# Banded self-attention in a decoder trunk: scores from split operands, transposes and values one tile further back, and the output projection's first tiles in two parts

## The chip, the core and the metric

The kernel runs on one core of a Trainium2 chip. Its engines take their instructions from queues of their own and wait for each other through semaphores: TensorE (PE in the profile; PEld are its weight loads) multiplies matrices into PSUM, VectorE (DVE), ScalarE (ACT) and GpSimd (POOL) work on tiles, and SyncE (SP) issues most of the transfers from memory. The metric is the time of one execution on the device in microseconds, here called us.

## The reference

A decoder trunk of two layers works on 256 positions of width 2048. Layer 0 mixes with a gated convolution and a state-space model; layer 1, the odd one, with the sliding-window attention below. After the mixer each layer has a cross-attention into 256 memory tokens and a gated MLP. Everything is float32. The change is in layer 1's mixer and in the table of its position bias:

```python
def swa_sink_attention(h, w_qkv, b_qkv, sinks, rel_bias, w_out):
    z = h @ w_qkv + b_qkv
    q, k, v = jnp.split(z, [N_Q_HEADS * HEAD_DIM, (N_Q_HEADS + N_KV_HEADS) * HEAD_DIM], axis=-1)
    ...
    kb, vb = with_prev(k), with_prev(v)
    s = jnp.einsum('bnqkgd,bnskd->bnkgqs', q, kb).astype(jnp.float32) * (HEAD_DIM ** -0.5)
    ...
    s = jnp.where(valid[None, :, None, None], s + bias[None, None], NEG_INF)
    ...
    p = jax.nn.softmax(jnp.concatenate([s, sink], axis=-1), axis=-1)[..., :-1]
    o = jnp.einsum('bnkgqs,bnskd->bnqkgd', p.astype(vb.dtype), vb)
    return o.reshape(Bsz, L, N_Q_HEADS * HEAD_DIM) @ w_out
```

There are 32 query heads of width 64 and 4 key heads. Queries come in two blocks of 128. A query sees the block of keys it is in and the block before, and of these the 128 latest positions. The first block has no block before it. So a head needs scores of 128 by 256 for the second block and of 128 by 128 for the first, 384 columns in all. A learned sink per head adds one more term to the softmax's sum.

## The kernel before

**Activations** lie with their features on the 128 partitions: a tensor of width 2048 is 16 tiles (KT = 16) of 128 features by 256 positions (T = 256).

**Split products.** A large product in float32 is made of three cheaper ones. Each operand is written as a high part in the type float32r and a low part, the rest. For weights `wload` loads a raw tile (L82, SyncE's queue, three buffers), ScalarE makes the high part of up to 1024 columns at a time (L90) and VectorE the low part (L91), with four buffers each. An activation tile `op` holds its high and its low half side by side (512 columns; `split`, L74 and L75, or `split_gain`, L67 and L68). For each k-tile `mm_hi` multiplies the weight's high part with all 512 columns (L105), and `mm_lo` the low part with the high half, 256 columns (L110). The two halves of the result bank are added later.

**`gemm`** runs over output tiles of 128 features. `start` loads a tile's weights and issues its matmuls: all of `mm_hi`, then the function `half`, then all of `mm_lo`. `finish` calls `evac`, which takes the result out of PSUM, and then the function `after`. With `pre` and `late` the first `pre` tiles leave their last `late` k-tiles for afterwards, which `held` collects. What `half`, `after` and `end` issue is wedged into the stream of matmuls at these places. The order on each engine is that of the program as far as the planner of the tile framework keeps it: it puts ready work ahead of work that waits.

**The odd mixer** (`odd_mixer`) first makes keys `kT` (two tiles; `evac_k` adds the bias on ScalarE, L690) and values `vt` (L719). Then a `gemm` over 16 q tiles makes two query heads in each. Its `evac_q` adds the two halves (L160 on ScalarE, L161 on VectorE), multiplies with the normalisation on GpSimd (L726), and adds the bias on ScalarE (L728), with the positions of each block in reverse order, so that a bias row can be read at a shifting offset. For each pair of heads j there are three steps:

- `scores(j)`: loads the bias from a table in memory (L737), 256 columns of each head; multiplies q and k as plain float32, 64 rows of the array for each head, with 256 columns for the second block (L742) and 128 for the first (L745), into two small banks; adds the bias on VectorE in four pieces (L747, L748); makes the softmax: maxima, exponentials on ScalarE with their sums (L757, L760), the sum with the sink (L761), its reciprocal (L762) and four multiplications with it (L765). The result is `s`.
- `transp(j)`: three transposes for each head on TensorE (L774) into two small banks, copied by ScalarE to `pT` (L777).
- `values(j)`: multiplies `vt` with `pT` in plain float32, 64 columns of the array for each head (L788), into a small bank, which `split` makes the next operand of `o_ops` (L789).

In q tile n, `half` issues `transp(n - 3)`, and `after` issues `scores(n - 1)` and `values(n - 3)`. Each plain float32 product is two instructions in the trace.

**The output projection** is a `gemm` over 16 tiles whose k-tiles are the 16 entries of `o_ops`. At its start 13 entries are there. `transp(13)` is issued ahead of it; its first three tiles hold back their last three k-tiles, and in them the dictionaries `halves` and `ends` issue what is left: `values(13)` and `scores(15)`, `transp(14)`, `values(14)`, `transp(15)`, `values(15)`. Its `evac` (`resid_evac`) adds both halves to the residual stream on VectorE (L288, L289), squares on ScalarE (L174), sums on GpSimd (L172), and splits the result for the next stage (L67, L68).

**The position bias** is made once, long before (`rel_bias_setup`): a row of 384 for each head, written to memory by one transfer (L676). A query's bias is a stretch of 256 of that row, at an offset that moves with the query.

**PSUM** is two pools of four banks each: `pp` for the results of `gemm` (the tag `ps`), `pm` for the small ones (`bank()`).

Of the kernel before, what the change touches and what calls it, by code (L numbers as in the profile page):

```python
# [22 lines left out]
P = 128  # L23
# [13 lines left out]
class Trunk:  # L37
# [623 lines left out]
    def rel_bias_setup(self):  # L661

        nc, I = self.nc, self.I
        with self.tc.tile_pool(name="rb", bufs=1) as pool:
# [10 lines left out]
            self.fd = self.dp.tile([32, 384], F32, name="fd")  # L675
            nc.scalar.dma_start(self.fd, f)  # L676

    def odd_mixer(self, xs):
# [3 lines left out]
        with tc.tile_pool(name="att", bufs=2) as pool:  # L682
            kT = [pool.tile([P, T], F32, name=f"kT{j}", tag=f"kT{j}", bufs=1) for j in range(2)]
            vt = pool.tile([P, 2, T], F32, name="vt", tag="vt", bufs=1)

            def evac_k(n, ps):
                z = self.t1()
                self.add_halves(z, ps)
                nc.gpsimd.tensor_tensor(z, z, self.rbc, op=ALU.mult)
                nc.scalar.activation(kT[n], z, AF.Identity, bias=self.k_b[:, n:n + 1])  # L690
# [32 lines left out]
            def evac_q(n, ps):  # L723
                z = self.t1()
                self.add_halves(z, ps)
                nc.gpsimd.tensor_tensor(z, z, rbc, op=ALU.mult)  # L726
                q = pool.tile([P, T], F32, name="q", tag="q", bufs=3)
                nc.scalar.activation(q.rearrange("p (b i) -> p b i", b=2)[:, :, ::-1], z.rearrange("p (b i) -> p b i", b=2), AF.Identity, bias=self.q_b[:, n:n + 1])  # L728
                qs[n] = q
# [3 lines left out]
            def scores(j):  # L733
                q = qs.pop(j)
                k = kT[j // 8]
                bias = pool.tile([P, 2, T], F32, name="bias", tag="bias", bufs=3)
                nc.sync.dma_start(bias, AP(tensor=self.fd.tensor, offset=self.fd.offset + 2 * j * 384, ap=[[1, P], [384, 2], [1, T]]))  # L737
                s = pool.tile([P, 2, 384], F32, name="s", tag="s", bufs=3)
                ps = [self.bank() for _ in range(2)]
                for hd in range(2):  # L740
                    r = slice(64 * hd, 64 * hd + 64)
                    nc.tensor.matmul(ps[hd][:, 0:T], lhsT=q[r, P:], rhs=k[r, :], start=True, stop=True)  # L742
                for hd in range(2):
                    r = slice(64 * hd, 64 * hd + 64)
                    nc.tensor.matmul(ps[hd][:, T:T + P], lhsT=q[r, :P], rhs=k[r, :P], start=True, stop=True)  # L745
                for hd in range(2):
                    v.scalar_tensor_tensor(s[:, hd, :T], ps[hd][:, :T], 0.125, bias[:, hd, :], op0=ALU.mult, op1=ALU.add)  # L747
                    v.scalar_tensor_tensor(s[:, hd, T:], ps[hd][:, T:T + P], 0.125, bias[:, hd, P:], op0=ALU.mult, op1=ALU.add)  # L748
# [13 lines left out]
                v.reciprocal(de, de)  # L762
                for hd in range(2):
                    for blk, sl in ((0, slice(0, T)), (1, slice(T, 384))):
                        v.tensor_scalar(s[:, hd, sl], s[:, hd, sl], de[:, blk, hd:hd + 1], None, op0=ALU.mult)  # L765
# [15 lines left out]
            def values(j):  # L781
                pts = sm.pop(j)
                po = self.bank()
# [7 lines left out]
            def after(n):  # L791
                if n >= 1:
                    scores(n - 1)
                if n >= 3:
                    values(n - 3)

            def half(n):
                if n >= 3:
                    transp(n - 3)
            self.gemm(lambda n: I["od_q"][n], range(16), xs, KT, evac_q, half=half, after=after)  # L800
            evac, nxt = self.resid_evac(G_XA + 1)
            halves = {0: lambda: (values(13), scores(15)), 1: lambda: values(14), 2: lambda: transp(15)}
            ends = {0: lambda: transp(14), 1: lambda: None, 2: lambda: values(15)}
            transp(13)
            self.gemm(lambda n: I["od_w_out"][n], range(16), _Lazy(o_ops), KT, evac, late=3, pre=3, half=lambda n: n in halves and halves[n](), end=lambda n: ends[n]())
# [296 lines left out]
```

## Time and profile before

| | |
|---|---|
| median of three runs | 2818.43 us |
| the three runs | 2815.97, 2818.43, 2819.57 us |
| the profiled execution, its own time | 2817.71 us |
| its span, from the first to the last instruction | 2815.9 us |
| granted TensorE clock, mean | 0.997 |
| the odd mixer's q tiles, from the first scores on | 1646.2 to 1764.8 us of the span |
| its first three output tiles | 1764.9 to 1788.6 us |
| transfers of od_w_out | 16 of 1024 KB, 4.8 us each to landing |

The profile is one execution. Between the span and the execution's own time lie 1.8 us in which no instruction of the program runs. A row of the costliest groups gives line, engine, operation, output from inputs, shapes and count, then the busy time, the mean nanoseconds of one, and the idle time of the engine just before, with what ended it. A row of the chain of waits gives start, length and what; the lengths add up to the time that passes.

### The profile page before, as it was taken

To read this page: it belongs to the slowest core of one execution; us is meant where nothing else is said; L and a number is where in the kernel's file an instruction comes from. 1 tells how busy PE (TensorE), PEld (TensorE's weight loads), DVE (VectorE), ACT (ScalarE), POOL (GpSimd) and SP (SyncE) were. 2 spreads that over 40 slices of the span, in tenths; PEclk is the share of its full clock that TensorE was granted. 3 is DMA by queue.
4 is the path that set the end of the run, shared out by engine and by line. 5 is a ranking of instruction groups with operands and counts; after the bars stand their busy time and mean duration, and the time that the engine had idled before them with its cause. 6 is when DMAs were issued, how large, how long until landed. Compare 5 with 4: busy or idle time off the path is not lost.

```text
span 2815.9 us, 42249 instructions
## 1 busy us (share of the span) xinstructions
PE 2785.6 (99%) x16263; PEld 2438.2 (87%) x16263; DVE 1975.3 (70%) x3227; ACT 1570.8 (56%) x2544; POOL 360.5 (13%) x397
## 2 busy tenths in 40 slices
PE   9999999999999999999999999999999999999998
PEld 8787878888988888888888888889888888888887
DVE  8978788867666666666666778776666666666666
ACT  7676766655555545545445566555555455454454
POOL 2000000000012211202112310000122022021122
PEclk9999999999999999999999999999999999999999
DMA  8664665555455545455454544454455554554544
GB/s 305 204 213 172 213 226 202 201 181 210 180 177 186 193 171 212 169 206 190 169 210 176 198 171 163 150 211 179 174 185 190 174 205 168 209 192 168 206 171 143
DMA packets 89788, 536.63 MB, mean 191 GB/s; under 512 B 10641, under 2 KB 17137, under 8 KB 38641
## 3 DMA queue, kind: packets, MB, share of 16 engines
q1 hardware_dynamic: 86656, 524.66, 52.7%
q10 hardware_dynamic: 2928, 9.26, 0.9%
q8 instruction: 127, 2.08, 0.3%
q14 instruction: 77, 0.62, 0.1%
HBM read 523.35 MB, written 10.53 MB: 190 GB/s over the span
## 4 chain that ended last, share of the span: by engine, by line
PE 94%; DVE 3%; ACT 2%; DMA 1%; issue 1%; POOL 0%; SPq 0%; DVEq 0%; ACTq 0%; POOLq 0%
PE ps L105 55%; PE ps L110 29%; PE ps L319 2%; PE ps L324 2%; PE ps L320 2%; DVE lo L91 1%; PE m L882 1%; PE m L788 1%; ACT stmp L489 1%; ACT hi L90 1%; DMA kv<-kst 0%; PE m L774 0%; DVE S L494 0%; PE m L742 0%; PE m L852 0%
## 5 line engine op out<-in xcount | busy, mean ns | idle before, releaser
L105 PE MATMUL ps<-op,hi 128*128 128x512 f32 x6997 | 1689.3, 392 | 5.4 <-ACT hi L90 2.8
L105 PEld LDWEIGHTS ps<-op,hi 128*128 128x128 f32 x6997 | 1283.2, 188 | 260.5 <-ACT hi L90 5.2
L91 DVE TENSOR_TENSOR lo<-raw,hi 128x1024 fp32r<-128x1024 f32 (+2 forms) x1033 | 1200.6, 1185 | 378.4 <-ACT hi L90 154.8
L90 ACT CAST hi<-raw 128x1024 fp32r<-128x1024 f32 (+2 forms) x1033 | 1001.8, 983 | 813.0 <-PE ps L105 720.5
L110 PEld LDWEIGHTS ps<-op,lo 128*128 128x128 f32 x7008 | 903.6, 191 | 38.5 <-DVE lo L91 2.3
L110 PE MATMUL ps<-op,lo 128*128 128x256 f32 x7008 | 920.5, 283 | 1.3 <-DVE lo L91 1.3
L172 POOL TENSOR_TENSOR acc<-acc,t 128x256 f32<-128x256 f32 x98 | 90.8, 927 | 1185.7 <-ACT t L174 1181.7
L160 ACT COPY t<-ps 128x256 f32<-128x256 f32 x290 | 106.9, 370 | 166.5 <-PE ps L110 163.6
L919 POOL TENSOR_TENSOR t<-t,rbc 128x256 f32<-128x256 f32 x88 | 68.8, 781 | 748.7 <-DVE t L161 720.9
L922 DVE SCALAR_TENSOR_TENSOR t<-t,ff_conv 128x255 f32<-128x255 f32 x88 | 42.9, 487 | 141.9 <-ACT t L921 141.9
L925 POOL TENSOR_TENSOR t<-t,rbc 128x256 f32<-128x256 f32 x88 | 109.5, 1244 | 216.2 <-ACT t L924 216.2
L68 DVE SCALAR_TENSOR_TENSOR op<-h,gains,op 128x256 fp32r<-128x256 f32 x96 | 72.8, 765 | 85.1 <-ACT op L67 85.0
L489 ACT ACTIVATE stmp<-S,s_pw 128x256 f32<-128x256 f32 (+3 forms) x256 | 116.8, 522 | 27.6 <-DVE S L496 21.6
L75 DVE TENSOR_TENSOR op<-t,op 128x256 fp32r<-128x256 f32 x104 | 43.8, 425 | 118.6 <-ACT op L74 118.2
L161 DVE TENSOR_TENSOR t<-ps,t 128x256 f32<-128x256 f32 x250 | 103.8, 415 | 0.9 <-ACT t L160 0.9
L319 PE MATMUL ps<-hi,op 128*128 128x512 f32 x256 | 101.0, 394 | 0.3 <-ACT hi L90 0.2
L320 PE MATMUL ps<-hi,op 128*128 128x512 f32 x256 | 99.8, 390 | 0.0
L931 POOL TENSOR_TENSOR t<-t 128x256 f32<-128x256 f32 x88 | 67.2, 764 | 135.0 <-DVE t L161 134.7
L74 ACT CAST op<-t 128x256 fp32r<-128x256 f32 x104 | 41.9, 406 | 50.7 <-POOL t L931 43.3
L494 DVE TENSOR_TENSOR S<-S,stmp 128x512 f32<-128x512 f32 (+11 forms) x92 | 60.6, 663 | 13.0 <-ACT stmp L489 12.8
L324 PE MATMUL ps<-lo,op 128*128 128x512 f32 x256 | 63.6, 390 | 0.7 <-DVE lo L91 0.7
L921 ACT ACTIVATE t<-t,ff_b,ff_conv 128x256 f32<-128x256 f32 x88 | 52.3, 595 | 20.7 <-POOL t L919 20.7
(213 smaller groups left out, 1494.9 us busy)
## 6 DMA issues: line engine op xcount, KB each, us to landing
raw<-in_ff_gate SPq DMA_DIRECT2D x88, 1024.0 KB, 4.8
raw<-in_ff_up SPq DMA_DIRECT2D x88, 1024.0 KB, 4.8
raw<-in_ff_down SPq DMA_DIRECT2D x128, 704.0 KB, 4.0
raw<-in_xa_k SPq DMA_DIRECT2D x32, 1024.0 KB, 4.9
raw<-in_xa_v SPq DMA_DIRECT2D x32, 1024.0 KB, 5.3
raw<-in_xa_q SPq DMA_DIRECT2D x32, 1024.0 KB, 4.8
raw<-in_xa_o SPq DMA_DIRECT2D x32, 1024.0 KB, 4.8
raw<-in_ev_w_in SPq DMA_DIRECT2D x28, 1024.0 KB, 4.9
```

What stands on the lines that cost most here:

```text
L90: nc.scalar.copy(hi, s)
L91: nc.vector.tensor_tensor(lo, s, hi.bitcast(F32), op=ALU.subtract)
L105: nc.tensor.matmul(ps, lhsT=hi, rhs=o, start=k == 0, stop=False)
L110: self.nc.tensor.matmul(ps[:, :T], lhsT=w[k][1], rhs=ops[k][:, :T], start=False, stop=k == K - 1)
L160: self.nc.scalar.copy(t, ps[:, T:])
L161: self.nc.vector.tensor_tensor(out, ps[:, :T], t, op=ALU.add)
L172: nc.gpsimd.tensor_tensor(self.acc, self.acc, self.sq, op=ALU.add)
L319: nc.tensor.matmul(ps[b], lhsT=o[:, b * P:(b + 1) * P], rhs=w[j][0], start=k == 0, stop=False)
L320: nc.tensor.matmul(ps[b], lhsT=o[:, T + b * P:T + (b + 1) * P], rhs=w[j][0], start=False, stop=False)
L324: nc.tensor.matmul(ps[b], lhsT=self.memop[k][:, b * P:(b + 1) * P], rhs=w[j][1], start=False, stop=k == KT - 1)
L489: nc.scalar.activation(tmp[:, x, :, p - p0, :], at(0, both, p), AF.Copy, scale=pw[:, x, k, 8 * b + p:8 * b + p + 1])
L925: nc.gpsimd.tensor_tensor(y, y, self.rbc, op=ALU.mult)
```

## The change

- `rel_bias_setup` writes the bias table with three stretches of 256 for each head instead of one row of 384, one for each 128 columns of scores, with three transfers.
- Keys and queries get a low half: after ScalarE's addition of the bias, which now writes float32r, VectorE computes the rest (`scalar_tensor_tensor`). The reversal of the positions moves from the output of that addition to its input.
- `scores` loads 384 columns of bias for each head (three runs of 128 for a partition and head instead of one of 256). It multiplies in three float32r passes, high with high, high with low, low with high, for each of the two blocks and both heads in turn: six matmuls of 256 columns and six of 128, instead of two and two float32 ones. The bias is added in one operation for each head.
- The softmax's normalisation is one multiplication over both heads, with the reciprocals laid out in a small tile `rd` (two reciprocals and a copy), instead of one reciprocal and four multiplications. `s` has four buffers instead of three.
- `values` takes its bank from `pp` instead of `pm`.
- In q tile n, `half` issues `transp(n - 4)` and `after` `values(n - 5)`; at the end 11 entries of `o_ops` are there.
- The output projection's first six tiles run in two `gemm` calls: first over 11 k-tiles, with the rest of the transposes, scores and values wedged in, each tile's result added to the residual stream by `resid_part` (two additions on VectorE); then over the other 5 k-tiles with the full `evac`. The last ten tiles run as before. Nothing is held back.

```diff
-            self.fd = self.dp.tile([32, 384], F32, name="fd")
-            nc.scalar.dma_start(self.fd, f)
+            self.fd = self.dp.tile([32, 3, 256], F32, name="fd")
+            for c, off in enumerate((0, P, P)):
+                nc.scalar.dma_start(self.fd[:, c, :], f[:, off:off + 256])
...
-            kT = [pool.tile([P, T], F32, name=f"kT{j}", tag=f"kT{j}", bufs=1) for j in range(2)]
+            kT = [pool.tile([P, 2, T], F32R, name=f"kT{j}", tag=f"kT{j}", bufs=1) for j in range(2)]
...
-                nc.scalar.activation(kT[n], z, AF.Identity, bias=self.k_b[:, n:n + 1])
+                b = self.k_b[:, n:n + 1]
+                nc.scalar.activation(kT[n][:, 0, :], z, AF.Identity, bias=b)
+                v.scalar_tensor_tensor(kT[n][:, 1, :], z, b, kT[n][:, 0, :].bitcast(F32), op0=ALU.add, op1=ALU.subtract)
...
-                q = pool.tile([P, T], F32, name="q", tag="q", bufs=3)
-                nc.scalar.activation(q.rearrange("p (b i) -> p b i", b=2)[:, :, ::-1], z.rearrange("p (b i) -> p b i", b=2), AF.Identity, bias=self.q_b[:, n:n + 1])
+                q = pool.tile([P, 2, 2, P], F32R, name="q", tag="q", bufs=3)
+                b = self.q_b[:, n:n + 1]
+                z2 = z.rearrange("p (b i) -> p b i", b=2)[:, :, ::-1]
+                nc.scalar.activation(q[:, 0], z2, AF.Identity, bias=b)
+                v.scalar_tensor_tensor(q[:, 1], z2, b, q[:, 0].bitcast(F32), op0=ALU.add, op1=ALU.subtract)
...
-                bias = pool.tile([P, 2, T], F32, name="bias", tag="bias", bufs=3)
-                nc.sync.dma_start(bias, AP(tensor=self.fd.tensor, offset=self.fd.offset + 2 * j * 384, ap=[[1, P], [384, 2], [1, T]]))
-                s = pool.tile([P, 2, 384], F32, name="s", tag="s", bufs=3)
+                bias = pool.tile([P, 2, 384], F32, name="bias", tag="bias", bufs=3)
+                nc.sync.dma_start(bias.rearrange("p a (c i) -> p (a c) i", c=3), AP(tensor=self.fd.tensor, offset=self.fd.offset + 2 * j * 768, ap=[[1, P], [256, 6], [1, P]]))
+                s = pool.tile([P, 2, 384], F32, name="s", tag="s", bufs=4)
                 ps = [self.bank() for _ in range(2)]
+                for b, cols, n in ((1, slice(0, T), T), (0, slice(T, 384), P)):
+                    for x, y in ((0, 0), (0, 1), (1, 0)):
+                        for hd in range(2):
+                            r = slice(64 * hd, 64 * hd + 64)
+                            nc.tensor.matmul(ps[hd][:, cols], lhsT=q[r, x, b, :], rhs=k[r, y, :n], start=x == y, stop=x == 1)
                 for hd in range(2):
-                    r = slice(64 * hd, 64 * hd + 64)
-                    nc.tensor.matmul(ps[hd][:, 0:T], lhsT=q[r, P:], rhs=k[r, :], start=True, stop=True)
-                for hd in range(2):
-                    r = slice(64 * hd, 64 * hd + 64)
-                    nc.tensor.matmul(ps[hd][:, T:T + P], lhsT=q[r, :P], rhs=k[r, :P], start=True, stop=True)
-                for hd in range(2):
-                    v.scalar_tensor_tensor(s[:, hd, :T], ps[hd][:, :T], 0.125, bias[:, hd, :], op0=ALU.mult, op1=ALU.add)
-                    v.scalar_tensor_tensor(s[:, hd, T:], ps[hd][:, T:T + P], 0.125, bias[:, hd, P:], op0=ALU.mult, op1=ALU.add)
+                    v.scalar_tensor_tensor(s[:, hd, :], ps[hd][:, :384], 0.125, bias[:, hd, :], op0=ALU.mult, op1=ALU.add)
...
-                v.reciprocal(de, de)
-                for hd in range(2):
-                    for blk, sl in ((0, slice(0, T)), (1, slice(T, 384))):
-                        v.tensor_scalar(s[:, hd, sl], s[:, hd, sl], de[:, blk, hd:hd + 1], None, op0=ALU.mult)
+                rd = pool.tile([P, 2, 3], F32, name="rd", tag="rd", bufs=3)
+                v.reciprocal(rd[:, :, 2], de[:, 1, :])
+                v.reciprocal(rd[:, :, 0], de[:, 0, :])
+                v.tensor_copy(rd[:, :, 1], rd[:, :, 0])
+                s6 = s.rearrange("p a (c i) -> p (a c) i", c=3)
+                v.tensor_tensor(s6, s6, rd.rearrange("p a c -> p (a c)").unsqueeze(2).to_broadcast([P, 6, P]), op=ALU.mult)
...
-                po = self.bank()
+                po = self.pp.tile([P, 512], F32, name="ps", tag="ps")
...
-                if n >= 3:
-                    values(n - 3)
+                if n >= 5:
+                    values(n - 5)
...
-                if n >= 3:
-                    transp(n - 3)
+                if n >= 4:
+                    transp(n - 4)
...
-            halves = {0: lambda: (values(13), scores(15)), 1: lambda: values(14), 2: lambda: transp(15)}
-            ends = {0: lambda: transp(14), 1: lambda: None, 2: lambda: values(15)}
-            transp(13)
-            self.gemm(lambda n: I["od_w_out"][n], range(16), _Lazy(o_ops), KT, evac, late=3, pre=3, half=lambda n: n in halves and halves[n](), end=lambda n: ends[n]())
+            wout = I["od_w_out"]
+            halves = {0: lambda: transp(12), 1: lambda: transp(13), 3: lambda: transp(14), 4: lambda: transp(15)}
+            afters = {0: lambda: (values(11), scores(15)), 1: lambda: values(12), 2: lambda: values(13), 4: lambda: values(14), 5: lambda: values(15)}
+            self.gemm(lambda n: wout[n][:, :11, :], range(6), list(o_ops), 11, self.resid_part, half=lambda n: n in halves and halves[n](), after=lambda n: n in afters and afters[n]())
+            self.gemm(lambda n: wout[n][:, 11:, :], range(6), o_ops[11:], 5, evac)
+            self.gemm(lambda n: wout[n], range(6, 16), o_ops, KT, evac)
```

`resid_part` is in the kernel before already, for the MLP's partial sums:

```python
    def resid_part(self, n, ps):
        h = self.h[n]
        self.nc.vector.tensor_tensor(h, h, ps[:, T:], op=ALU.add)
        self.nc.vector.tensor_tensor(h, h, ps[:, :T], op=ALU.add)
```

## The prediction

> **What bounds the kernel now.** I read the page first (busy shares, then the costliest groups), then the chain of waits for the stage that the change touches, tile by tile, and last the timeline of one tile. All times are microseconds; a row of the chain is start, length, what.
>
> ```profile
> span 2815.9 us, 42249 instructions
> PE 2785.6 (99%) x16263; PEld 2438.2 (87%) x16263; DVE 1975.3 (70%) x3227; ACT 1570.8 (56%) x2544; POOL 360.5 (13%) x397
> ```
>
> TensorE is busy 99% of the span, so the change can gain only what it takes off TensorE's own stream, or lose what it makes TensorE wait. The stage is the odd layer's mixer: sixteen q tiles, then sixteen output tiles. This is the chain over one q tile in its steady state, and behind the "..." two plain output tiles' worth from the end of the stage:
>
> ```profile
> 1679.58 3.87 PE ps L105 x16
> 1683.45 0.66 PE m L774 x6
> 1684.10 1.91 PE ps L110 x16
> 1686.01 0.63 PE m L742 x4
> 1686.64 0.22 PE m L745 x4
> 1686.87 1.24 PE m L788 x12
> ...
> 1784.49 0.81 PE m L788 x12
> ...
> 1788.64 3.65 PE ps L105 x16
> 1792.30 1.91 PE ps L110 x16
> ```
>
> A plain tile costs 3.65 + 1.91 = 5.56. The q tile costs 8.53: the sum of its six rows. Beyond the plain tile these are 0.66 for transposes, 0.85 for scores, 1.24 for values, and 0.2 on the first row, since a plain matmul that follows values starts late (3.87 against 3.65). The same twelve value instructions take 0.81 at 1784.49, where their operands have long been there, and 1.24 in the q tile. The waits say why:
>
> ```profile
> L788 PEld LDWEIGHTS m<-pT,vt 128*64 128x64 f32 x192 | 12.7, 136 | 6.2 <-ACT pT L777 4.9 <-issue 1.0
> 1685.15 2.36 DVE L91 TENSOR_TENSOR lo<-raw,hi 128x1024 fp32r<-128x1024 f32 x2 [1.70 <-PE ps L110]
> 1686.35 0.83 ACT L777 COPY pT<-m 128x384 f32<-128x384 f32 x2
> 1686.86 1.24 PE L788 MATMUL m<-pT,vt 128*64 128x128 f32 x12
> ```
>
> TensorE transposes tile j at 1683.45 and wants its values at 1686.86; ScalarE makes the copy L777 only from 1686.35 to 1687.18, behind the exponentials of a later tile. The second head's copy is therefore late in every tile, and the two heads' value matmuls no longer run as pairs. VectorE and ScalarE are no bound on average: over the q tiles from the first scores on, VectorE is busy 95.44 and ScalarE 81.84 of 118.60 (the columns are stretch, length, then busy time of PE, PEld, DVE, ACT, POOL):
>
> ```profile
> 1646.20:1764.80 118.60, 118.32 (x803) 98.56 (x802) 95.44 (x264) 81.84 (x222) 10.35 (x14) 1.00 0.45 155
> 1764.80:1788.60 23.80, 23.71 (x160) 19.36 (x160) 14.61 (x46) 12.98 (x34) 0.73 (x1) 1.00 0.24 89
> ```
>
> **The change, part by part.** *Transposes and values a tile further back.* Values now read a copy that was made a whole tile earlier, about 8 before they need it. The wait goes: 1.24 - 0.81 = 0.43 a tile, in the 13 q tiles that hold values now (n = 3 to 15), 5.6 in all. Bounds: 0, if another wait takes its place, and 0.43 a tile. I take the whole, since the copy is late by less than 1 and gets 8. One further place goes with it: at 1678 the chain leaves TensorE altogether and runs through ScalarE, and the tile takes 1679.58 - 1670.78 = 8.80 against 8.53.
>
> ```profile
> 1670.78 3.86 PE ps L105 x16
> ...
> 1677.92 0.37 ACT pT L777
> ...
> 1678.33 1.24 PE m L788 x12
> ```
>
> That is 0.27 more, once. What is late next? The normalised scores, needed by the transposes, get a tile more too, and a fourth buffer `s` carries them. The value bank moves from the pool of four small banks (two for scores, two for transposes) to the pool of GEMM banks, which holds at most two live tiles and one value bank of its four. Neither becomes a bound.
>
> *Scores from split operands.* Now a head pair takes two fp32 instructions for 256 columns and two for 128: 0.63 + 0.22 = 0.85. After, it takes three passes of 256 and three of 128. No row has that shape with 128 columns. The nearest row is the state-space part's product, also fp32r operands on a slice of the array's rows, with several row groups side by side: six groups of four matmuls with 256 columns.
>
> ```profile
> 73.12 0.98 PE L388 MATMUL m<-us,BT 32*128 32x256 f32 x24
> 74.03 0.50 PE L105 MATMUL ps<-op,hi 128*128 128x512 f32 x1
> ```
>
> From the first start to the next work it takes 74.03 - 73.12 = 0.91 for six groups of 256. Three of them have 128 here, and a group of 128 columns with its weight load takes no less than the 0.66 / 6 = 0.11 of a transpose, against 1.91 / 16 = 0.12 for one of 256. So 0.91 - 3 x 0.01 = 0.88, say 0.87: 0.02 more than now, 0.3 over sixteen tiles. The ends are far apart. Below: if each group took only its share of passes, three for four, 0.85 x 3/4 = 0.64, a gain of 0.21 a tile, 3.4 in all. Above: if a narrow fp32r matmul ran like an fp32 one, a group of 128 would cost the 0.22 of L745's whole row, 3 x (0.22 - 0.11) = 0.33 more a tile, 5.3 in all. I take 0.87, by the row that is nearest in form.
>
> By the Trainium skill ("FP8 and Floating Point Precision", TensorE Precision Notes) a true fp32 product is four passes, H*H + H*L + L*H + L*L, so the three products of the split would save a quarter of the scores, and the sum would end near 2809. The trace agrees that an fp32 product is more than one pass (64 instructions on L742 for 32 products), but its 0.85 is already under the 0.91 of L388's six fp32r groups, so there a pass less saves nothing. It is kept as a rival below.
>
> *The other engines.* VectorE gets the low half of q (one operation like L841) and two more small ones like L762, while the four bias additions become two and the four normalisations one.
>
> ```profile
> L841 DVE TENSOR_TENSOR q<-t,q 128x256 fp32r<-128x256 f32 x32 | 13.4, 420 | 6.7 <-ACT q L840 6.7
> L747 DVE SCALAR_TENSOR_TENSOR s<-m,bias 128x256 f32<-128x256 f32 x32 | 12.9, 403 | 2.5 <-PE m L745 2.5
> L748 DVE SCALAR_TENSOR_TENSOR s<-m,bias 128x128 f32<-128x128 f32 x32 | 8.8, 276 | 0.0
> L765 DVE TENSOR_SCALAR s<-s,st 128x256 f32<-128x256 f32 x32 | 15.0, 470 | 0.0
> L765 DVE TENSOR_SCALAR s<-s,st 128x128 f32<-128x128 f32 x32 | 8.8, 276 | 0.0
> L762 DVE RECIPROCAL st<-st 128x4 f32<-128x4 f32 x16 | 2.7, 169 | 0.0
> L91 DVE TENSOR_TENSOR lo<-raw,hi 128x1024 fp32r<-128x1024 f32 x903 | 1129.8, 1276 | 375.7 <-PE ps L110 153.5 <-ACT hi L90 152.0 <-issue 33.6
> L91 DVE TENSOR_TENSOR lo<-raw,hi 128x384 fp32r<-128x384 f32 x128 | 70.7, 552 | 0.0
> ```
>
> Added: 0.42 + 2 x 0.17 = 0.76. Merged: 2 x (0.40 + 0.28) = 1.36 becomes 2 x 0.55 (384 wide, by L91) = 1.10, and 2 x (0.47 + 0.28) = 1.50 becomes one of 768, 0.98 by the straight line between L91's two widths. The sum is zero. VectorE stays at 95.44 / 118.60 x 8.53 = 6.9 of a tile of 8.1, 85%: hidden behind TensorE; without that cover each 0.1 a tile would cost 1.6. The low half adds a wait of its own: it stands in VectorE's queue behind ScalarE's high half, and behind it stand the bias additions; the scores need it only at the end of the next tile. The larger bias loads (384 KB instead of 256 KB, three times the runs, each half as long) stand on SyncE's queue ahead of a weight load.
>
> ```profile
> bias<-fd SPq DMA_DIRECT2D x16, 256.0 KB, 3.6
> L737 SPq DMA_DIRECT2D bias<-fd x16: 377/377/463, 794.0 to 1750.1; - x16
> L676 ACTq DMA_DIRECT2D fd<-f x1: 316/316/316, 673.0 to 673.0; - x1
> ```
>
> They took 3.6 to land; twice that is still under one tile, three are in flight, and the DMA share of the stretch is 0.45. I take nothing, and up to 1 as the upper end. Three writes instead of one at the bias setup go out on ScalarE's queue at 673, 0.3 each, and the first load of them follows at 794: nothing.
>
> *The output tiles in two parts.* Matmuls stay equal in number: 11 + 5 k-tiles for 16. The queue of work in the stretch of output tiles holds one transpose set and two value sets more than before, which the q tiles have less.
>
> ```profile
> 1764.88 0.90 PE ps L105 x3
> ```
>
> Before, the first three tiles' 23.76 (1764.88 to 1788.64) hold 3 x 5.56 for tiles, 1.97 for three transpose sets, 0.85 + 0.81 + 0.21 = 1.87 for scores and values with the late start behind them, 2 x 1.02 for two value sets with theirs, and 0.2 of the late start at its head: 22.8. Some 0.9 go to parts wedged into each other. With each part at a fixed place I take back 0.5 of it (bounds 0 and 0.9). Against it stands part two: six tiles of five k-tiles, 5/16 x 5.56 = 1.74 of TensorE each. For each one VectorE has 0.84 of L91 (640 columns, by the same line), two additions and a split:
>
> ```profile
> L288 DVE TENSOR_TENSOR h<-h,ps 128x256 f32<-128x256 f32 x95 | 39.2, 412 | 3.7 <-PE ps L110 3.7
> L68 DVE SCALAR_TENSOR_TENSOR op<-h,gains,op 128x256 fp32r<-128x256 f32 x96 | 72.8, 765 | 85.1 <-ACT op L67 85.0
> raw<-in_ff_down SPq DMA_DIRECT2D x128, 704.0 KB, 4.0
> raw<-in_od_w_out SPq DMA_DIRECT2D x16, 1024.0 KB, 4.8
> ```
>
> That is 0.84 + 0.82 + 0.77 = 2.43 against 1.74: VectorE falls behind by 0.7 a tile, 4.1 over six, if its durations add up. But four `lo` buffers let it have two to four tiles' weights ready, and additions may lag by the four banks (three tiles, 5.2). I take 0.4 for part two, most of it the wait for the last value tile's operand (bounds 0 and 4.1). The first part's twelve extra additions (0.41 each, 5) lie beside six tiles of 11/16 x 5.56 = 3.8 in which VectorE, at 14.61 of 23.80, has room. The twelve smaller loads land in about 4.0 or less, with three ahead.
>
> **The sum**, against the profiled execution (2817.71, span 2815.9): -5.6 - 0.27 - 0.5 + 0.3 + 0.4 = -5.7, so 2812.0. It lies 0.7 under the median of the three runs shown, 2818.43. On that median I forecast 2812.7.
>
> **Rivals.** *Narrow fp32r matmuls run like fp32* (for: no fp32r matmul in the trace has under 256 columns; against: 512 columns take 3.65 / 16 = 0.23 and 256 take 0.12, a straight line through nothing): +5.3, 2818.0. *VectorE paces part two*: up to +3.7 beyond my 0.4, about 2816. *The scores take three quarters*: -3.4 and the 0.3 that falls away, 2809.0. *The wait moves but stays*: the planner keeps L777 behind the exponentials so far that a tile's distance doesn't help; all 5.6 return, 2818.3. *Slower*: the low half of q is issued in VectorE's queue behind the pair of L91 that waits for L110. That pair starts at 1685.15 and ends at 1687.51, the low half 0.42 later, 1687.93, while the scores now start at 1686.01. TensorE would wait 1.9 a tile, 15 tiles, 29: 2841. It decides only if the low half is not issued before 1685.15; its high half is done 4 earlier, which speaks against it:
>
> ```profile
> 1680.23 0.51 ACT L728 ACTIVATE q<-t,q_b 128x256 f32<-128x256 f32 x1 [0.24 <-POOL t L726]
> ```
>
> **Chances.** Forecast 0.52, narrow matmuls 0.18, part two 0.12, three quarters 0.08, slower 0.06, wait stays 0.04. A measurement of this kernel can tell about 0.2% (5.6) from no change, so the border of faster is 2812.8, and my forecast sits on it. Of the forecast's 0.52 I put 0.32 below the border, with three quarters 0.08 and a little: faster 0.41. The rest of the forecast, narrow matmuls, part two and the staying wait: same 0.52. Slower 0.07. The range reaches from three quarters to the two cases that give the gain back: 2808.8 to 2818.3.
>
> **What would show it.** Right: L788's row loses its wait on L777, the q tiles with values shrink from 8.53 to 8.1, and the pieces for scores keep 0.8 to 0.9. Wrong: starts of the 128-column score groups 0.2 apart instead of 0.11; TensorE gaps at L105 or L110 in the six short tiles, ended by VectorE or ScalarE; a gap ahead of the scores ended by VectorE.

## The result and the profile after

The changed kernel takes 2832.48 us (median of 4 runs, 2832.15 to 2833.27) against 2817.88 us for the kernel before: a ratio of 1.0052, 95% interval 1.0035 to 1.0070. The change costs 14.6 us where 5.7 were forecast as a gain. It is slower, and outside the range.

The page, beside the two lines shown of before:

```profile
span 2830.6 us, 42368 instructions
PE 2788.1 (99%) x16327; PEld 2442.9 (86%) x16327; DVE 1987.9 (70%) x3215; ACT 1568.8 (55%) x2550; POOL 364.1 (13%) x397
```

TensorE is busy 2788.1 instead of 2785.6, while the span grew by 14.7. So, against the kernel before, most of the new time is idle time of TensorE. The busy time by stretch shows where: first the q tiles, then the six short output tiles (stretch, length, busy time of PE, PEld, DVE, ACT, POOL, then the granted clock, the DMA share and GB/s).

```profile
1640.10:1783.60 143.50, 130.22 (x917) 111.25 (x916) 108.81 (x259) 85.06 (x238) 16.08 (x16) 0.95 0.44 145
1783.60:1819.50 35.90, 35.90 (x239) 30.93 (x238) 23.69 (x51) 17.47 (x39) 0.91 (x1) 1.00 0.52 153
```

The short output tiles are full. In the q tiles TensorE is idle for 13 of 143.5 and its clock falls to 0.95. VectorE, at 108.81, isn't busy all the time either. The chain of waits, which ran through TensorE before, leaves it at 1644.74 and comes back at 1778.01. This is one turn of it:

```profile
1735.81 0.44 DVE t L161
...
1736.38 0.75 POOL t L730
1737.15 0.52 ACT q L735
1737.69 0.48 DVE q L736
1738.18 0.60 DVE st L757
...
1739.50 1.14 DVE lo L91
...
1741.44 1.27 ACT s L766 x6
1742.82 1.22 DVE lo L91
...
1744.42 0.31 DVE s L773
...
1745.30 0.43 DVE t L161
```

It goes from VectorE's sum of the halves (L161) through GpSimd, ScalarE's q and VectorE's low half (L736) to the maxima, through ScalarE's exponentials (L766), VectorE's normalisation, and back to L161. Both weight pieces (L91) stand in this chain, one ahead of the exponentials and one behind them. One turn takes 1745.30 - 1735.81 = 9.49; the q tile took 8.53 before and was forecast at 8.1. No step of it is TensorE's. The waits of the stretch name the same steps (engine, line and tile that waits, what ended the wait; us in total, times, longest):

```profile
ACT q L735 <- POOL t L730: 29.6, 15, 2.8
ACT s L766 <- DVE st L761: 20.4, 11, 1.9
DVE st L767 <- ACT s L766: 15.9, 12, 1.8
DVE q L736 <- ACT q L735: 11.2, 13, 1.5
...
PE m L752 <- DVE s L754: 8.6, 4, 3.0
...
PE ps L105 <- DVE op L75: 3.8, 1, 3.8
```

ScalarE waits for VectorE, and VectorE for ScalarE, in turn: two engines that work one after the other. TensorE's 8.6 ahead of the scores (L752) are waits for its small banks, which the additions of the tile before (L754) free too late; 3.8 more come at the first output tile. VectorE's own queue over that turn shows what changed (start, length, what, and in brackets the idle time before it and what ended it). First the exponentials of the kernel before, which ran from 1684.60 to 1686.44, beside its pair of L91 from 1685.15 to 1687.51; then the changed kernel:

```profile
1684.60 0.49 ACT L760 ACTIVATE s<-s,st 128x256 f32<-128x256 f32 x1
...
1686.26 0.18 ACT L760 ACTIVATION_READ_ACCUMULATOR s<-s,st 128x1 f32 x1
```

```profile
1736.15 1.01 DVE L754 SCALAR_TENSOR_TENSOR s<-m,bias 128x384 f32<-128x384 f32 x2
1737.69 0.48 DVE L736 SCALAR_TENSOR_TENSOR q<-t,q_b,q 128x256 fp32r<-128x256 f32 x1 [0.53 <-ACT q L735]
1738.09 0.68 DVE L757 TENSOR_REDUCE st<-s 128x2 f32<-128x512 f32 x1
...
1739.42 1.22 DVE L91 TENSOR_TENSOR lo<-raw,hi 128x1024 fp32r<-128x1024 f32 x1
...
1742.74 0.17 DVE L767 TENSOR_TENSOR st<-st 128x4 f32<-128x4 f32 x1 [1.83 <-ACT s L766]
1742.82 1.22 DVE L91 TENSOR_TENSOR lo<-raw,hi 128x1024 fp32r<-128x1024 f32 x1
```

Before, both weight pieces (L91, x2 in one row of the prediction) stood together between the maxima and the sum (then L761, now L767), and VectorE had 2.36 of work to do beside and behind ScalarE's exponentials. Now one piece stands among the small operations ahead of the exponentials, which wait for it, and one behind the sum. During the exponentials VectorE has nothing to do (the 1.83 in brackets). The traces of the kernels below show the same: in the steady q tiles VectorE's queue has two pieces between the maxima and the sum, or one and three in turn, in the kernels under 2820, and at most one in those over 2828. The kernel whose order is held by hand stands between the two.

What the change does on TensorE itself came out as forecast. From the same chain, behind its return to TensorE:

```profile
1782.80 0.83 PE m L752 x12
...
1788.33 0.81 PE ps L797 x12
...
1812.50 1.15 PE ps L105 x5
1813.65 0.59 PE ps L110 x5
```

The scores take 0.83 (forecast 0.87, before 0.85), the values 0.81 (before 1.24), a tile of part two 1.15 + 0.59 = 1.74, with no gap.

### The profile page after: what moved, and what is told of

The parts are those of the page before. It is cut to its first block, busy times and chain, and to the rows that moved or that the text cites. A ratio compares the mean times of both kernels' runs of the same rounds, so it can differ in the third digit from the quotient of the medians.

```text
span 2830.6 us, 42368 instructions
## 1 busy us (share of the span) xinstructions
PE 2788.1 (99%) x16327; PEld 2442.9 (86%) x16327; DVE 1987.9 (70%) x3215; ACT 1568.8 (55%) x2550; POOL 364.1 (13%) x397
## 4 chain that ended last, share of the span: by engine, by line
PE 89%; DVE 5%; ACT 4%; issue 1%; POOL 1%; DMA 0%; SPq 0%; DVEq 0%; ACTq 0%; POOLq 0%
PE ps L105 53%; PE ps L110 28%; PE ps L319 2%; PE ps L320 2%; PE ps L324 2%; DVE lo L91 2%; ACT stmp L489 1%; ACT hi L90 1%; PE m L894 1%; ACT s L766 1%; POOL t L730 0%; DVE S L494 0%; DVE s L773 0%; DVE s L754 0%; DVE st L757 0%
## 5 line engine op out<-in xcount | busy, mean ns | idle before, releaser
L105 PE MATMUL ps<-op,hi 128*128 128x512 f32 x6997 | 1692.5, 392 | 9.3 <-DVE op L75 4.9
L105 PEld LDWEIGHTS ps<-op,hi 128*128 128x128 f32 x6997 | 1285.2, 189 | 265.8 <-DVE op L75 6.2
L91 DVE TENSOR_TENSOR lo<-raw,hi 128x1024 fp32r<-128x1024 f32 (+3 forms) x1039 | 1202.7, 1179 | 358.7 <-ACT hi L90 163.1
L90 ACT CAST hi<-raw 128x1024 fp32r<-128x1024 f32 (+3 forms) x1039 | 1001.9, 978 | 781.6 <-PE ps L105 684.2
L160 ACT COPY t<-ps 128x256 f32<-128x256 f32 x290 | 106.8, 370 | 165.5 <-PE ps L110 162.6
L75 DVE TENSOR_TENSOR op<-t,op 128x256 fp32r<-128x256 f32 x104 | 43.9, 425 | 118.7 <-ACT op L74 118.3
L161 DVE TENSOR_TENSOR t<-ps,t 128x256 f32<-128x256 f32 x250 | 103.8, 415 | 2.3 <-ACT t L160 2.3
```

The lines of the kernel that those rows point to most:

```text
L90: nc.scalar.copy(hi, s)
L91: nc.vector.tensor_tensor(lo, s, hi.bitcast(F32), op=ALU.subtract)
L105: nc.tensor.matmul(ps, lhsT=hi, rhs=o, start=k == 0, stop=False)
L160: self.nc.scalar.copy(t, ps[:, T:])
L161: self.nc.vector.tensor_tensor(out, ps[:, :T], t, op=ALU.add)
```

## The experiments

The theories have letters in what was expected. **A**: the low half of q on VectorE; A1 by its work and its wait in the queue, A2 because the scores read it and so hang on a ring through three engines (later called D). **B**: the softmax's new pieces. **C**: the distances of transposes and values. **O**: the order in which the planner lays the queues. **P**: the matmuls of the third product themselves. In the diffs `low(q)` stands for the line that makes q's low half.

**Which part of the change.** Four runs. Plain float32 scores in the changed kernel, as before:

```diff
-    low(q)
...
-    nc.tensor.matmul(ps[hd][:, cols], lhsT=q[r, x, b, :], rhs=k[r, y, :n], start=x == y, stop=x == 1)
...
+    nc.tensor.matmul(ps[hd][:, 0:T], lhsT=q[r, P:], rhs=k[r, :], start=True, stop=True)
...
+    nc.tensor.matmul(ps[hd][:, T:T + P], lhsT=q[r, :P], rhs=k[r, :P], start=True, stop=True)
```

> The changed kernel with plain float32 scores again: keys and queries have no low half, everything else of the change stays (bias layout, one normalisation, lags, value bank, output tiles in two parts). Theory A, the low half of q on VectorE closes a loop of waits (L161, GpSimd's product, ScalarE's bias, the low half, the bias additions, the exponentials, the sum, back to L161) that paces the q tiles at 9.5 instead of 8.5: the loop opens, q tiles near 8.1, 2812 to 2815. Rival B, the rearranged softmax (one normalisation with three small operations ahead) is what holds VectorE: unchanged, 2830 to 2833. Rival C, the lags alone make the planner order the queues badly: unchanged too, 2830 to 2833.

Measured 2811.63, ratio 0.9977 [0.9968, 0.9986]: the whole loss is gone, and the kernel is faster than the one before. TensorE is busy all of a stretch of the q tiles, with VectorE at 84%:

```profile
1660.00:1760.00 100.00, 100.00 (x708) 85.19 (x706) 83.62 (x204) 70.63 (x202) 10.27 (x13) 1.00 0.52 172
```

The low half on GpSimd, from a second copy that ScalarE makes:

```diff
-    v.scalar_tensor_tensor(q[:, 1], z2, b, q[:, 0].bitcast(F32), op0=ALU.add, op1=ALU.subtract)
+    nc.scalar.activation(zb2, z2, AF.Identity, bias=b)
+    nc.gpsimd.tensor_tensor(q[:, 1], zb2, q[:, 0].bitcast(F32), op=ALU.subtract)
```

> The changed kernel with the low half of q made on GpSimd (which is idle most of the time) from a second ScalarE copy, instead of on VectorE. Theory A in its narrow form (only VectorE's wait for the low half counts, 0.5 to 1.2 a tile, and its 0.48 of work): 2817 to 2820. Theory A in its wide form (every wait in VectorE's queue that no ready work covers counts; here the order of the queue has nothing between the maxima and the sum of the exponentials, so about 2 a tile stay): q tiles 8.8 to 9.0, 2823 to 2827. Rivals B and C: 2830 and more.

Measured 2833.33, 1.0055 [1.0039, 1.0072]. Both forms of A missed: without VectorE's operation the time stays. (The edit also gives ScalarE a second copy to make, and puts GpSimd between ScalarE and the scores. The time is the one put down for B and C, which the run before had already spoken against.)

The old pieces of the softmax (four additions, one reciprocal, four multiplications) in the changed kernel:

```diff
-    s6 = s.rearrange("p a (c i) -> p (a c) i", c=3)
...
+    v.tensor_scalar(s[:, hd, sl], s[:, hd, sl], de[:, blk, hd:hd + 1], None, op0=ALU.mult)
```

> The changed kernel with the softmax as before: four bias additions and one reciprocal with four multiplications; split scores, lags and output tiles stay changed. Theory A: the loop stays, VectorE's busy time is about the same, 2829 to 2836. Rival B: 2812 to 2818.

Measured 2835.75, 1.0062 [1.0047, 1.0077]. B falls.

The split scores alone in the kernel before:

```diff
+    low(q)
...
+    for b, cols, n in ((1, slice(0, T), T), (0, slice(T, 384), P)):
+        for x, y in ((0, 0), (0, 1), (1, 0)):
...
```

> The kernel before with the split scores alone: low halves of keys and queries and the three passes, nothing else changed. Theory A: slow as the changed kernel or slower, since values wait for their copy as well, 2830 to 2840. Rivals B and C: 2817 to 2820, the scores' own cost being equal.

Measured 2835.56, 1.0064 [1.0049, 1.0079]. The split brings the loss alone; C falls.

**What in the split.** The low half issued half a tile later, in `half` instead of `evac_q`:

```diff
-    low(q)
...
+    if n >= 1:
+        low(n - 1)
```

> The changed kernel with the low half of q still on VectorE, but issued half a tile later, ahead of the next tile's transposes; the scores still read it. In the order of VectorE's queue it now stands behind the maxima, where its operands are long there, and nothing stands between the maxima and the sum of the exponentials. Theory A1 (VectorE's own wait for the low half, 0.5 to 1.2 a tile, is what paces): the wait goes, q tiles 8.1 to 8.3, 2812 to 2816. Theory A2 (the whole round through the queues of VectorE, GpSimd and ScalarE paces, each wait in it that no ready work covers counts, and in this order the exponentials' 2.0 is uncovered): q tiles 8.8 to 9.2, 2822 to 2829.

Measured 2832.89, 1.0047 [1.0030, 1.0063]: nothing gained, where A1 and A2 both had a gain.

Plain scores (as in the first run), with the same VectorE operation and wait, into a buffer that nobody reads:

```diff
...
+    dl = pool.tile([P, 2, P], F32, name="dl", tag="dl", bufs=2)
+    v.scalar_tensor_tensor(dl, z.rearrange("p (b i) -> p b i", b=2), self.q_b[:, n:n + 1], q.rearrange("p (b i) -> p b i", b=2)[:, :, ::-1], op0=ALU.add, op1=ALU.subtract)
```

> e1 (plain float32 scores) with an operation on VectorE like the low half, from the same operands after ScalarE's bias, written to a buffer that nothing reads. The planner puts it behind two bias additions and the normalisation, and keeps both L91 between the maxima and the sum. Theory A1 (the operation's work and wait on VectorE pace the tile): 2822 to 2832. Theory A2 (only an order with uncovered waits paces; here the operation's wait is covered by 2.2 of other work and the exponentials by the pair of L91): as e1, 2811 to 2814.

Measured 2812.93, 0.9980 [0.9970, 0.9989]. Operation and wait cost about 1 (against 2811.63 without them), hidden as the prediction had it. A1 falls.

The split without q's low half; the product of it with the keys' high half is left out:

```diff
-    for x, y in ((0, 0), (0, 1), (1, 0)):
+    for x, y in ((0, 0), (0, 1)):
...
-    low(q)
```

> The changed kernel without the low half of q: the scores take two float32r passes (high with high, high with low), so the third product is left out. Theories A1 and A2: the round through GpSimd and ScalarE into VectorE is open, q tiles at or under 8.1; the scores are a third shorter (0.87 to 0.64, 16 times: 3.7), 2807 to 2811. Rival D, the float32r passes themselves or the keys' split bring the slow order: 2825 and more.

Measured 2810.12, 0.9971 [0.9960, 0.9982]. I took it for a proof of A2. It wasn't: the run takes away the reading of the low half and the third product at once.

The distances and the output tiles in two parts, alone in the kernel before:

```diff
-    s = pool.tile([P, 2, 384], F32, name="s", tag="s", bufs=3)
+    s = pool.tile([P, 2, 384], F32, name="s", tag="s", bufs=4)
...
-    po = self.bank()
+    po = self.pp.tile([P, 512], F32, name="ps", tag="ps")
...
-    values(n - 3)
+    values(n - 5)
...
-    transp(n - 3)
+    transp(n - 4)
...
+    self.gemm(lambda n: wout[n][:, 11:, :], range(6), o_ops[11:], 5, evac)
...
```

> The kernel before with the lags, the fourth buffer of s, the value bank and the output tiles in two parts alone: scores, bias layout and softmax as before. By the terms of the prediction (-5.6 for the values' wait, -0.27 once, -0.5 in the first output tiles, +0.4 in the second part) 2812.4; with e1 at 2811.6 this says what the rearranged softmax and bias are worth: as e1 within 1.5 if they are worth nothing, 2815 and more if they carry a part of e1's gain.

Measured 2812.03, 0.9977 [0.9968, 0.9986]: -6.3 against the before of the same runs (2818.34).

**Reading or third product.** These four split what the run without the low half had mixed. The first holds VectorE's order by hand, with all of the changed kernel's arithmetic. `norm` is the sum with what follows it, and the pinned sum stays behind what VectorE was given before it:

```diff
-    v.tensor_tensor(de, sums, es, op=ALU.add)
...
     if n >= 4:
+        norm(n - 4)
         transp(n - 4)
...
+    tc.keep_in_program_order(v.tensor_tensor(de, sums, es, op=ALU.add))
```

> All of the changed kernel's arithmetic, with the low half of q and three products. Only the softmax's sum and what follows it (reciprocals, normalisation) are issued later, and the sum is held on VectorE's queue behind the low parts of the weights of the q tile four further on, so that in the queue the pair of weight pieces (L91) stands between the maxima and the sum, as it does in the kernel before. Theory O (the order that the planner gives VectorE's queue is the cause; nothing that the change computes is too dear): the exponentials and the low half have the pair of weight pieces to hide behind, TensorE is busy all the time again in the q tiles, the tile takes 8.1, and the time is 2811 to 2815 us. Theory D (the data dependence scores <- VectorE's low half <- ScalarE's q is the cause, whatever the order): the round through GpSimd, ScalarE and VectorE stays, 2824 to 2836 us.

Measured 2826.60, 1.0030 [1.0018, 1.0041]: between the two, about 6 better than the changed kernel. That lies in the range put down for D and outside the one for O. The timeline of one turn:

```profile
1694.74 1.05 ACT L90 CAST hi<-raw 128x1024 fp32r<-128x1024 f32 x1
...
1695.69 0.37 ACT L160 COPY t<-ps 128x256 f32<-128x256 f32 x1
1695.83 1.22 DVE L91 TENSOR_TENSOR lo<-raw,hi 128x1024 fp32r<-128x1024 f32 x1 [1.66 <-ACT hi L90]
...
1698.30 0.51 ACT L735 ACTIVATE q<-t,q_b 128x256 fp32r<-128x256 f32 x1 [2.25 <-POOL t L730]
...
1698.86 1.19 PE L752 MATMUL m<-kT,q 64*128 64x256 f32 x12 [0.52 <-ACT q L735]
```

ScalarE still makes a weight piece (L90) ahead of L160, VectorE's L91 waits for that piece ahead of L161, and so q comes 0.52 too late for the scores. Over its q tiles TensorE waits 3.6 for q in seven tiles, and 5.1 at the first output tile. One queue was held; the other kept its order: in ScalarE's queue one cast L90 stands ahead of the exponentials and one behind the copies, as in the changed kernel, while the kernel before has both ahead of the exponentials. That ScalarE's order makes up the rest was not tried.

Three products, but no low half; the third is high with high again instead of low with high:

```diff
-    for x, y in ((0, 0), (0, 1), (1, 0)):
+    for p, (x, y) in enumerate(((0, 0), (0, 1), (0, 0))):
...
-    low(q)
```

> The changed kernel without the low half of q; three float32r products are still issued, the third being high with high again, so the scores are not the reference's. Theory O: the planner counts the third product's time on TensorE as it does in the changed kernel and leaves the weight pieces at one between the additions and one beside the sum, so most of the loss stays though nothing reads a low half: 2818 to 2832 us, a little less than the changed kernel because ScalarE's q no longer has VectorE behind it. Theory D: without a low half there is no round; as with two products, 2810 to 2813 us.

Measured 2828.92, 1.0037 [1.0023, 1.0051]. No low half is made, and most of the loss is there (10.7 over the kernel before in the same runs), with its waits between the same two engines (100 us of the q tiles):

```profile
ACT q L735 <- POOL t L730: 27.8, 11, 2.8
DVE st L766 <- ACT s L765: 18.3, 10, 2.0
...
PE m L751 <- ACT q L735: 8.9, 7, 1.4
```

Two products, of which one reads the low half (the product with the keys' low half is left out):

```diff
-    for x, y in ((0, 0), (0, 1), (1, 0)):
+    for x, y in ((0, 0), (1, 0)):
```

> The changed kernel with two products only: high with high, and the low half of q with the high half of the keys; the product with the keys' low half is left out. The scores do read what VectorE makes after ScalarE. Theory O: with two products the planner lays both weight pieces between the maxima and the sum, so it is fast, and the scores are a third shorter: 2808 to 2813 us. Theory D: the low half is read, so the round stays, 2825 to 2835 us.

Measured 2813.48, 0.9982 [0.9973, 0.9991]. Of TensorE's waits one is left, 3.4 at the first output tile (L105 for L75's operand).

And plain scores that read a copy which VectorE makes behind ScalarE's q:

```diff
...
+    v.tensor_copy(q, q0)
```

> The kernel with plain float32 scores, with q copied once more by VectorE behind ScalarE's addition of the bias, and the scores reading the copy: the dependence of the low half without the split products. Theory O: the order of the queue stays as with plain scores, 2811 to 2815 us. Theory D: as slow as the changed kernel, 2826 to 2836 us.

Measured 2812.75, 0.9981 [0.9972, 0.9990]. So the scores may read what VectorE makes last, at no cost. A2 and D fall with these three runs; what counts is the third product.

**Order or matmul.** One width changed in the changed kernel: the first block's products are 256 columns wide instead of 128, with the added columns read by nobody.

```diff
-    for b, cols, n in ((1, slice(0, T), T), (0, slice(T, 384), P)):
+    for b, cols, n in ((1, slice(0, T), T), (0, slice(T, 512), T)):
```

> The changed kernel with one number changed: the three products for the first block of queries are 256 columns wide like those of the second, not 128. The extra 128 columns of the bank are read by nobody, so TensorE has more work: 3 more column groups of 128 a tile, at the some 0.01 each of the prediction 0.03 a tile, 0.5 in all. With this width the planner lays VectorE's queue as in the kernel before (both weight pieces between the maxima and the sum). Theory O (the planner takes a narrow float32r product for dearer than a wide one and so orders the queues for a TensorE that is slower than it is; the order makes the loss): fast again, 2811 to 2815 us, TensorE's gaps gone, tile 8.1 to 8.2. Theory P (the third product's matmuls themselves, narrow ones in three passes, hold something up on the chip: weights, banks, or the reads of the low half): more of the same work, 2830 to 2836 us.

Measured 2813.95, 0.9986 [0.9977, 0.9995]. TensorE has more to do, and the kernel is 18.5 faster than with narrow products. Its chain over one q tile:

```profile
1708.25 3.85 PE ps L105 x16
1712.11 0.66 PE m L782 x6
1712.76 1.91 PE ps L110 x16
1714.67 0.91 PE m L752 x12
1715.58 0.81 PE ps L797 x12
1716.39 3.88 PE ps L105 x16
```

It is TensorE's again: 1716.39 - 1708.25 = 8.14 a tile, with 0.91 for the wide scores instead of 0.83. VectorE's queue in this tile:

```profile
1710.60 0.47 DVE L736 SCALAR_TENSOR_TENSOR q<-t,q_b,q 128x256 fp32r<-128x256 f32 x1
1711.00 0.68 DVE L757 TENSOR_REDUCE st<-s 128x2 f32<-128x512 f32 x1
...
1713.81 2.36 DVE L91 TENSOR_TENSOR lo<-raw,hi 128x1024 fp32r<-128x1024 f32 x2 [1.01 <-PE ps L110]
1716.09 0.16 DVE L767 TENSOR_TENSOR st<-st 128x4 f32<-128x4 f32 x1
```

The pair of weight pieces is back between the maxima and the sum, and the one wait is for TensorE. In ScalarE's queue, too, both casts L90 stand ahead of the exponentials again. The low half and its three products are all there.

The same widening where the split is the only change:

```diff
-    for b, cols, n in ((1, slice(0, T), T), (0, slice(T, 384), P)):
+    for b, cols, n in ((1, slice(0, T), T), (0, slice(T, 512), T)):
```

> The same widening in the kernel before with the split scores alone (which took 2835.6). Theory O: the order of the kernel before comes back, with its distances and its wait of the values: 2817 to 2821 us. Theory P: 2833 to 2838 us.

Measured 2817.73, 0.9999 [0.9990, 1.0008], against 2835.56 with narrow products: the split alone costs nothing once the products are wide. The pair of L91 is back in its queue as well. So P falls, twice, as far as it means the third product's work. The widening takes away the narrowness together with the order, so by itself it can't tell whether narrow products alone hold something up on the chip. Against that speak the narrow scores' 0.83 beside the wide ones' 0.91, and the kernels with two products (2810.12 and 2813.48), whose first block is narrow too.

## Why the prediction was wrong

- **The values' wait** (-5.6): right. Values take 0.81 in the chain, and the tile of the widened kernel takes 8.14 against the 8.1 forecast for narrow scores.
- **The distances and output tiles together**: right. Without the scores' 0.3 the terms come to -6.0; measured alone they give -6.3. Only the sum was timed. Inside it, the chain shows part two to cost nothing where 0.4 was put (1.74 a tile, no gap), so the rival in which VectorE paces part two is false. A wait that the sum did not have stands at the first output tile, for its last operand: 3.8 in the changed kernel, and 3.4 in the one with two products that read the low half, whose q tiles have no such ring; so the ring is not its only cause.
- **The scores on TensorE** (0.87): right, 0.83. So the rival of narrow products that run like float32 (0.87 + 0.33 = 1.20) is false on the chip, and three quarters (0.64) is false too.
- **The normalisation and VectorE's sum of zero**: right in time, not in work. The distances with the old softmax and scores take 2812.03, with the new softmax 2811.63. VectorE's busy time by the pages is 1980.0 and 1979.2 in these two, and 1986.4 in the widened kernel with all parts: some 0.4 a tile more where zero was put. In the widened kernel it is hidden.
- **The step that failed** is the next sentence of that part: VectorE "stays at 95.44 / 118.60 x 8.53 = 6.9 of a tile of 8.1, 85%: hidden behind TensorE". It takes the order of the queues from before and puts new durations in it. Work of 6.9 hides in a tile of 8.1 only as long as VectorE and ScalarE work beside each other. With the changed scores the planner laid the queues anew, so that in the turn shown no weight piece is left beside the exponentials; VectorE fell to 108.81 of 143.50, 76%, and was the pace all the same, by its waits. The price is a turn of 9.49 instead of 8.1.
- **The slower rival** named the place (a gap ahead of the scores, VectorE's queue at the pair of L91) but not the mechanism. It let the low half stand behind the pair. In the runs the low half's position, work and reading cost nothing; the pair itself was pulled apart.
- **How the loss adds up.** The changed kernel's span is 18.8 over that of the widened one (2830.6 and 2811.8). By the pages TensorE is busy 2788.1 in the one and 2781.8 in the other, which has more columns to do. So 6.3 of the 18.8 is busy time, which goes with the granted clock of 0.95 in the changed kernel's q tiles, and the other 12.5 is idle time. The waits shown above make 8.6 + 3.8 = 12.4; the widened kernel has 1.1 at the same first output tile.

That the order is the cause is shown by the widened kernels (same steps, more matmul columns, another order, and the loss is gone), by the chain of the changed kernel, which runs through the reordered steps and not through TensorE, and by the kernels' queues, in which the weight pieces stand apart where the time is lost. The one run that changes the order and keeps three narrow products gives back 5.9 of it, with one queue held; that the other queue's order is worth the rest is not shown. Why the planner orders so is inferred. Three narrow products (beside the three wide ones of the second block) turn it, two narrow or three more wide ones do not; so it seems to take a narrow float32r product for dearer than a wide one, and to plan for a TensorE that is slower than the real one. Its prices are in no trace. Open is also what of ScalarE's order made the rest of the loss where only VectorE's was held.

## What to carry to other kernels

Where a planner lays the queues, the cost of an edit is not only its instructions: a matmul's shape alone (here 128 columns or 256) can reorder engines that the edit hardly touches. So after an edit compare the order of the queues first, above all what stands between a long operation and the one that waits for it, and hold a fast variant against a slow one with as few differences as can be. An engine at 76% can be the pace, if it and another one wait for each other in turn. And a run that takes two things away at once, such as an operand and the product that reads it, tells neither apart.

## What the runs showed of the hardware

GpSimd's product L730 takes twice its time when VectorE's weight piece runs beside it. Two timelines of the changed kernel, first beside the additions, then beside L91:

```profile
1736.38 0.74 POOL L730 TENSOR_TENSOR t<-t,rbc 128x256 f32<-128x256 f32 x1 [8.19 <-DVE t L161]
...
1755.11 1.22 DVE L91 TENSOR_TENSOR lo<-raw,hi 128x1024 fp32r<-128x1024 f32 x1
1755.34 1.57 POOL L730 TENSOR_TENSOR t<-t,rbc 128x256 f32<-128x256 f32 x1 [8.75 <-DVE t L161]
```

It takes 0.74 beside the additions (L754, which ran from 1736.15) and 1.57 where it starts 0.23 into L91: 0.83 more, where L91 has 0.99 left. In five of the changed kernel's sixteen q tiles it takes 1.52 to 1.59, in four of them beside an L91 right behind L161, in the fifth beside the multiplication L773, whose inputs also both lie in SBUF; in the kernel before all sixteen take 0.73 to 0.75. So this is part of several turns of the ring. By the Trainium skill ("SBUF — State Buffer", Who interferes with whom) a VectorE instruction with both inputs in SBUF shuts out a GpSimd instruction that reads SBUF until it ends, and one with a single SBUF input does not; the trace agrees with both.

A gap also costs TensorE's clock behind it. Three rows of the timeline, and two stretches of ten:

```profile
1729.87 1.27 PE L752 MATMUL m<-kT,q 64*128 64x256 f32 x12 [2.96 <-DVE s L754]
...
1732.34 5.04 PE L105 MATMUL ps<-op,hi 128*128 128x512 f32 x16
...
1741.52 3.92 PE L105 MATMUL ps<-op,hi 128*128 128x512 f32 x16
```

```profile
1726.00:1736.00 10.00, 7.02 (x43) 5.58 (x42) 7.65 (x19) 5.62 (x16) 1.57 (x1) 0.83 0.43 144
1736.00:1746.00 10.00, 10.00 (x76) 8.63 (x75) 7.54 (x19) 5.62 (x16) 0.88 (x2) 1.00 0.36 115
```

Behind an idle time of 2.96 the granted clock is 0.83 in the stretch, and the sixteen matmuls of L105 take 5.04 instead of 3.92, so that one gap costs over 1 more than its own length. In steps of two the clock is 0.50 from 1732 to 1734. From the q tiles to the first output tile the changed kernel has five gaps of over 1 ahead of a matmul: behind those of 1.29 and 1.84 the clock stays at 1.00, behind those of 2.52, 2.96 and 3.83 it falls to 0.50. By the Trainium skill ("TensorE: Matmul & The Clock Gate", The HAM clock gate) the clock halves after an idle window of some 3.4; here 2.52 was enough.
